# Layer 0's experts in 12 groups instead of 13, the crowded-expert branch in the first group, and the sort in front of the first gather

## Chip, core and metric

The kernel runs on one core of a Trainium2 chip. The metric is device time in microseconds (us) for one execution of the whole program, which computes a two-layer trunk in one launch. Engines are named as in the profile: PE (TensorE matmul), PEld (its weight loads), DVE (VectorE), ACT (ScalarE), POOL (GpSimd) and SP (SyncE, which here issues the DMAs of the weights). A name with a q, as SPq, is the engine's instruction sequencer.

## What is computed

The trunk has two layers. Each layer has a mixer (layer 0: convolution beside differential attention; layer 1: gated linear attention) and then a hierarchical mixture of experts. Layer 0 treats 512 tokens (256 latent, 256 context), layer 1 only the 256 latent ones. The change lies in the mixture of layer 0. Cut to what matters, the reference is

```python
lg = xt @ rg_w + rg_b                       # 4 expert groups
gi = top1(lg); pg = softmax(lg)[gi]
le = (xt @ re_w + re_b)[:, gi, :]           # 8 experts in the chosen group
top_v, top_i = top_k(le, 2)
gate = pg * softmax(top_v)
expert = 8 * gi + top_i                     # two of 32 experts for each token
for e in range(32):                         # rows of e: the tokens routed to it
    h = silu(x_e @ w1[e]) * (x_e @ w3[e])   # w1, w3: 1024 x 512
    y_e = h @ w2[e]                         # w2: 512 x 1024
y[token] += gate * y_e
```

So layer 0 has 1,024 rows to distribute over 32 experts, and every expert's three matrices of 2 MB each (float32) must be read once, whatever number of rows it has.

## The kernel before

**Groups.** The experts of layer 0 are worked off in groups that fill 128 rows. `GROUPS[0]` lists the widths: `PAIR` is two experts of 64 rows, `MIX` is 64, 32 and 32, `QUAD` is four of 32, and one group is (96, 32). There are 13 groups: PAIR, PAIR, (96, 32), MIX, PAIR, MIX, PAIR, MIX, PAIR, MIX, PAIR, MIX, MIX. The first four experts (`E0 = 4`) keep their own numbers, so that their weights can be loaded before the routing is known. The other 28 are sorted by their number of rows, and the widest places go to the fullest experts. Layer 1 has eight groups, all QUAD. A group's width is split into parts (in `parts`): 64 columns in a PAIR, 32 in all others. A matmul of a part uses only the columns of the PE array that belong to it, and parts can run side by side.

**Crowded experts.** An expert with more rows than its place has is finished in a loop, 32 rows in a pass: `rest()` reads the number of passes (`nri`) on every engine, and branches over the loop if it is zero. `crowded()` computes `nri`; in layer 0 it calls `sort()`, which ranks the experts and reorders the table `tab` (slot numbers, gates, counts, expert numbers) with PE transposes and matmuls. `rest()` runs in group `REST[0] = 3`, counted from 0, after that group's down product, whose result is scattered first. Group 0 needs nothing of the sort: its positions `pos0` come from the routing.

**One group.** For group j the program says: `up` (lines 1520 to 1528: x times w1 and w3, 16 steps over k, each with one matmul per part), then the rest of the group's loads, then `act_h` (silu, gate at line 1440, product, four PE transposes), then `prep` of group j + 1 (`group_hot`, `gather`, `gates`: a 0/1 matrix times the tokens, transposed), then `scatter` of group j - 1 (line 1463 on PE, lines 1467 and 1468 on DVE and POOL), then `slots_T` of j + 1, then `down` (lines 1530 to 1537: h times w2), then the first loads of group j + 1, then `split_y`.

**Ring.** A tile of weights is 128 x 2048 float32, 1 MB; an expert has six. `wtile()` hands out places of a ring: four base tiles of the pool `ring` (named wt in the profile), nine that `open_ring` adds and one that `more_ring` adds (wx), 14 in layer 0. The pool has one tag `wt` with four buffers. From the 120th tile on, the index is shifted by one place (`TURN`). The loop body's six loads take six places too, whether it runs or not. `load_group` is a generator: it issues the w1 and w3 loads of a group at its first two steps (four per expert), and the two w2 loads per expert when the caller runs it to its end, after `up`. For sorted experts it first reads the expert's number from `numi` into an SP register (line 1494); lines 1481 and 1483 issue the load for a fixed and for a sorted expert.

**Order.** `TileContext(nc, schedule_with_timeline_sim=True)` lets a planner order the instructions of each engine: by program order as priority, but by its own estimate of when each instruction's inputs are there. So it may put a later group's gather between the matmuls of an up product, or take the parts of a step apart. Nothing is moved over a branch: what the program says before `rest()` stands before it on every engine. Each engine's instructions run in the order in which they were put. `later()` lowers the priority of what stands in it.

**Ahead of the groups.** The last blocks of tokens are modulated by `modulate(b, True)` for b = 2 and 3: ACT, POOL, ACT, and then the low half XL of the split (line 1230), for b = 2 on POOL and for b = 3 on DVE. The routing's DVE chain (lines 1279 to 1338) runs at the same time.

Of the kernel before, what the change touches and what calls it, by code (L numbers as in the profile page):

```python
# [9 lines left out]
FT = mybir.dt.float32  # L10
# [8 lines left out]

D = 1024  # L20
RING = 4
TURN = (120, 1)
LATE = (9, 11)
MORE = (1, 2)

# [1 line left out]

E0 = 4
PAIR, MIX, QUAD = (64, 64), (64, 32, 32), (32,) * 4
GROUPS = ((PAIR, PAIR, (96, 32), MIX, PAIR, MIX, PAIR, MIX, PAIR, MIX, PAIR, MIX, MIX), (QUAD,) * 8)  # L30
REST = (3, 1)
EPS = 1e-6
NE = 32
LAMBDA_INIT = 0.8 - 0.6 * math.exp(0.0)
# [47 lines left out]
def trunk_kernel(ctx: ExitStack, tc: tile.TileContext, A: dict, out: bass.AP):  # L82
    nc = tc.nc
    const = ctx.enter_context(tc.tile_pool(name="const", bufs=1))
    ring = ctx.enter_context(tc.tile_pool(name="ring", bufs=RING))
    psum = ctx.enter_context(tc.tile_pool(name="psum", bufs=1, space=PSUM))
    dram = ctx.enter_context(tc.tile_pool(name="dram", bufs=1, space=bass.MemoryType.DRAM))
    late, ring_at, ring_of = [], [0], []

    def pool(es, name, side):  # L90
        return es.enter_context(tc.tile_pool(name=name, bufs=1, side=side, reuse_waits="tile"))
# [19 lines left out]
    def wtile():  # L111

        if not late:
            return ring.tile([128, 2048], FT, name="wt", tag="wt")
        f = late[(ring_at[0] + TURN[1] * (ring_of[1] == "ring0" and ring_at[0] >= TURN[0])) % len(late)]
        ring_at[0] += 1
        return f()

    def open_ring(es, name, side, n, more=(), order=None):

        f = [lambda: ring.tile([128, 2048], FT, name="wt", tag="wt")] * RING
        for i in range(n):
            p = pool(es, f"{name}{i}", side)
            f.append(lambda p=p: p.tile([128, 2048], FT, name="wx"))
        f += [lambda m=m: m for m in more]
        ring_of[:] = es, name, side
        late[:] = [f[i] for i in order] if order else f
        ring_at[0] = 0
        es.callback(late.clear)
# [1000 lines left out]
    def moe_open(l, nb, side, X):  # L1130
# [88 lines left out]
        def modulate(b, last=False):  # L1219

            x = xs[b]
            if last:
                nc.scalar.activation(x, x, AF.Copy, scale=rs[:, b:b + 1])
                nc.gpsimd.tensor_add(x, x, B2[:, b // 2])
            else:
                nc.vector.scalar_tensor_tensor(x, x, rs[:, b:b + 1], B2[:, b // 2], op0=OP.mult, op1=OP.add)
            t = slice(b * 128, (b + 1) * 128)
            xv = x.rearrange("p (i k) -> p k i", k=8)
            nc.scalar.activation(X[0][:, :, t], xv, AF.Copy)
            (nc.gpsimd if last and b % 2 == 0 else nc.vector).tensor_sub(X[1][:, :, t], xv, X[0][:, :, t].bitcast(FT))  # L1230

        return dict(l=l, nb=nb, ns=ns, es=es, es1=es1, mp=mp, rp=rp, side=side, tab=tab, sub16=sub16, lg=lg, route=route, route_end=route_end, modulate=modulate, X=X, more=[], rs=rs, B2T=B2T if l else None)

    def moe(M):
# [15 lines left out]
        with es:  # L1250
# [93 lines left out]
            with es2:  # L1344
# [141 lines left out]
                def load_group(g):  # L1486

                    W = {}
                    es_ = []
                    p0, m, _ = g  # L1490
                    for x in range(m):
                        e = p0 + x
                        if l == 0 and e >= E0:
                            e = nc.values_load(numi[0:1, e:e + 1], engines=SPE, min_val=0, max_val=NE - 1)
                        es_.append(load_expert(W, e, x))
                    for i, _ in enumerate(zip(*es_)):
                        if i in (0, 4):
                            yield W
                    for i in es_:
                        next(i, None)  # L1500
                    yield W
# [13 lines left out]
                def prep(g, P):  # L1515
                    xgT = ep.tile([128, 8, 128], FT, name="xgT", tag="xgT", bufs=1)
                    gather(P, xgT)
                    return xgT, P, gates(P, g)
# [25 lines left out]
                def sort():  # L1544

                    key, kp, mine = sm[:, 0], sm2[:, 0:1], sm2[:, 1:2]
                    nc.vector.tensor_scalar(num, rev32, -1.0, float(NE), op0=OP.mult, op1=OP.add)

                    nc.vector.scalar_tensor_tensor(key, cnt, 32.0, rev32, op0=OP.mult, op1=OP.add)
                    nc.vector.tensor_scalar(key[:, 0:E0], rev32[:, 0:E0], 1e5, None, op0=OP.add)  # L1550
                    t = sm[:, 1]
                    nc.vector.tensor_mul(t, key, sel4)
                    nc.vector.reduce_sum(kp, t, axis=AX.X)
                    nc.vector.tensor_scalar(t, key, kp, None, op0=OP.is_gt)
                    nc.vector.reduce_sum(mine, t, axis=AX.X)

                    nc.vector.tensor_scalar(mine, mine, 1.0, None, op0=OP.add)
                    nc.vector.tensor_scalar(t, cst[:, C_RK:C_RK + NE], mine, None, op0=OP.is_equal)
                    row = sm2[:, 2:6]
                    nc.vector.reduce_sum(row, ident.rearrange("p (r e) -> p r e", e=NE), axis=AX.X)  # L1560
                    M = ep.tile([128, 512], FT, name="pm", tag="s", bufs=1)[:, 0:128].rearrange("p (r e) -> p r e", r=4)
                    nc.vector.tensor_tensor(M, t[:, None, :].to_broadcast([128, 4, NE]), row[:, :, None].to_broadcast([128, 4, NE]), op=OP.mult)
                    rows_ = 2 * nb + 2
                    tT = ep.tile([128, 512], FT, name="tT", tag="xg", bufs=1)
                    tp = trps()
                    for i in range(0, rows_, 4):
                        n = min(4, rows_ - i) * NE
                        nc.tensor.transpose(tp[0:n, i * 32:i * 32 + 128], tab[:, i:min(i + 4, rows_)].rearrange("p r e -> p (r e)"), ident)
                        nc.vector.tensor_copy(tT[0:n, i * 32:i * 32 + 128], tp[0:n, i * 32:i * 32 + 128])
                    tp = trps()  # L1570
                    for i in range(0, rows_, 4):
                        n = min(4, rows_ - i) * NE
                        nc.tensor.matmul(tp[:, i * 32:i * 32 + n], tT[0:n, i * 32:i * 32 + 128], M.rearrange("p r e -> p (r e)")[0:n, 0:n],
                                         start=True, stop=True)
                    nc.vector.tensor_copy(tab, tp[:, 0:rows_ * NE].rearrange("p (r e) -> p r e", e=NE))
                    nc.vector.tensor_copy(numi, num)
# [101 lines left out]
                def rest():  # L1678

                    n = nc.values_load(nri[0:1, 0:1], min_val=0, max_val=64)  # L1680
                    with tc.If(n > 0):
                        n2 = nc.values_load(nri[0:1, 0:1], min_val=0, max_val=64)
                        with tc.For_i(0, n2):
                            ei, pg = ov_pick()
                            e = nc.values_load(ei[0:1, 0:1], engines=SPE, min_val=0, max_val=NE - 1)
                            W = {}
                            for _ in load_expert(W, e, 1):
                                pass
                            pre = ov_gather(pg)
                            hT2 = ov_up(W, pre)  # L1690
                            scatter(pre[1], split_y(ov_down(W, hT2)))

                NG = len(groups)
                pr = prep(groups[0], group_hot(groups[0], pos0))
                nG = slots_T(pr[1])
                crowded()
                prev = None
                ld = load_group(groups[0])
                for _ in range(2):
# [1 line left out]
                for j, g in enumerate(groups):  # L1701
                    xgT, P, gc = pr
                    G = nG
                    hs = up(W, xgT, g)
                    for _ in ld:
                        pass
                    hT = act_h(hs[0], hs[1], gc)
                    if j + 1 < NG:
                        pr = prep(groups[j + 1], group_hot(groups[j + 1]))
                    if prev is not None:  # L1710
                        scatter(*prev)
                    if j + 1 < NG:
                        nG = slots_T(pr[1])
                    if j == REST[l] and l:
                        rest()
                    ys = down(W, hT, g)
                    if j + 1 < NG:
                        ld = load_group(groups[j + 1])
                        for _ in range(2):
                            W = next(ld)  # L1720
                    prev = (G, split_y(ys))
                    if j == REST[l] and l == 0:
                        scatter(*prev)
                        prev = None
                        rest()
                scatter(*prev)

    moe(mixer0())
# [26 lines left out]
```

## Time and profile before

| | us |
|---|---|
| median of three runs | 1575.86 (1575.17 to 1578.94) |
| the profiled execution | 1574.82 |
| its span | 1573.1 |
| mixer 0 and routing, about | 0 to 347 |
| groups of layer 0 and their scatter, about | 347 to 876 |
| mixer 1, about | 876 to 1140 |
| groups of layer 1, about | 1140 to 1573 |

The page gives the busy time of PE as 1331.3 us (85% of the span), of DVE as 674.0, of ACT as 369.0 and of POOL as 338.7. It moved 498.11 MB, a mean of 317 GB/s. Its second part cuts the span into 40 equal slices of 39.3 us; in the row of GB/s, layer 0's experts are the slices around 295, 400, 376, 213, 324 and then 420 to 424, and layer 1's are the last eleven, at 426 to 427. A busy PE is not PE at its peak.

### The profile page before, as it was taken

The page shows a single profiled execution, that of the slowest core. Times are in us where ns is not written, and L with a number is a line of the kernel's source. Part 1 is how long each engine was busy: PE and PEld are TensorE (multiplying, and loading weights), DVE is VectorE, ACT ScalarE, POOL GpSimd, SP SyncE. Part 2 cuts the span into 40 slices and gives each one's busy share as a digit, 9 for nine tenths or more (in the row PEclk, how much of TensorE's full clock was granted, in tenths as well). Part 3 has the DMA queues.
Part 4 walks back from the last instruction along what each step waited for, and adds up shares of the span by engine and source line. Part 5 has one row for each costly group of instructions (what it writes and reads, how often), then busy time and mean ns, then how long its engine had stood idle before and what let it go on. Part 6 is the DMA issues. An engine that isn't in the chain of part 4 may idle for free. (4 is left out here: it accounts for less than half of the span.)

```text
span 1573.1 us, 19365 instructions
## 1 busy us (share of the span) xinstructions
PE 1331.3 (85%) x7541; PEld 671.3 (43%) x7541; DVE 674.0 (43%) x1301; ACT 369.0 (23%) x706; POOL 338.7 (22%) x234
## 2 busy tenths in 40 slices
PE   5998989859997999999998799988776678778776
PEld 4765647643443434343332487776322122212211
DVE  4589885762245133334334838676202012102121
ACT  3255554531010100001001366444100000000000
POOL 1477402430012011111012545462000000000000
PEclk9999978889997999999999799999798899999998
DMA  9867162377995799999998824468599999999995
GB/s 315 297 222 256 53 215 58 102 299 295 400 376 213 324 422 423 422 423 422 422 404 293 319 88 161 164 216 321 236 426 426 427 427 427 427 427 426 427 427 240
DMA packets 100829, 498.11 MB, mean 317 GB/s; under 512 B 17605, under 2 KB 30248, under 8 KB 45948
## 3 DMA queue, kind: packets, MB, share of 16 engines
q1 hardware_dynamic: 96780, 490.37, 77.9%
q0 software_dynamic: 1680, 6.16, 1.2%
q8 instruction: 61, 1.00, 0.2%
q10 hardware_dynamic: 2272, 0.28, 0.1%
q14 instruction: 36, 0.29, 0.1%
HBM read 495.68 MB, written 1.10 MB: 316 GB/s over the span
## 5 line engine op out<-in xcount | busy, mean ns | idle before, releaser
L1526 PE MATMUL pj<-wx,xgT 128*32 128x512 f32 (+1 forms) x1616 | 330.9, 639 | 59.7 <-DMA wx<-in_moe_w_dram 56.7
L1468 POOL TENSOR_TENSOR H<-H,sc 128x512 f32<-128x512 f32 x68 | 86.7, 1275 | 899.1 <-DVE sc L1467 899.1
L1535 PE MATMUL pj<-wx,hT 128*32 128x512 f32 (+1 forms) x824 | 184.7, 608 | 5.0 <-ACT hT L1445 2.8
L1440 DVE SCALAR_TENSOR_TENSOR s<-s,gc,pj 128x512 f32<-128x512 f32 x21 | 15.7, 747 | 399.6 <-PE pj L1526 328.4
L1526 PEld LDWEIGHTS pj<-wx,xgT 128*32 128x32 f32 (+1 forms) x1616 | 79.8, 120 | 249.0 <-issue 137.8
L1526 PE MATMUL pj<-wt,xgT 128*32 128x512 f32 (+1 forms) x648 | 151.5, 603 | 18.4 <-DMA wt<-in_moe_w_dram 17.7
L370 POOL TENSOR_TENSOR wl<-wt,wh 128x1024 fp32r<-128x1024 f32 x50 | 126.8, 2543 | 144.0 <-ACT wh L369 135.4
L289 PE MATMUL pj<-wh,XH 128*128 128x512 f32 x304 | 123.7, 418 | 15.2 <-ACT p L621 6.8
L290 PE MATMUL pj<-wl,XH 128*128 128x512 f32 x304 | 124.2, 409 | 1.6 <-POOL wl L370 1.6
L1467 DVE TENSOR_TENSOR sc<-wk,g 128x512 f32<-128x512 f32 x136 | 87.6, 686 | 85.5 <-PE wk L1463 83.7
L291 PE MATMUL pj<-wh,XL 128*128 128x512 f32 x304 | 123.6, 408 | 0.2
L1535 PEld LDWEIGHTS pj<-wx,hT 128*32 128x32 f32 (+1 forms) x824 | 44.1, 115 | 94.1 <-issue 81.6
L369 ACT ACTIVATE wh<-wt 128x1024 fp32r<-128x1024 f32 x66 | 69.3, 1056 | 54.4 <-PE pj L291 35.4
L1468 DVE TENSOR_TENSOR H<-H,sc 128x512 f32<-128x512 f32 x68 | 79.6, 1171 | 2.0
L289 PEld LDWEIGHTS pj<-wh,XH 128*128 128x128 f32 x304 | 59.0, 195 | 44.1 <-issue 10.1
L1526 PEld LDWEIGHTS pj<-wt,xgT 128*32 128x32 f32 (+1 forms) x648 | 38.6, 117 | 90.4 <-issue 56.9
L1439 ACT ACTIVATE s<-pj 128x512 f32<-128x512 f32 x21 | 12.5, 597 | 252.4 <-PE pj L1526 245.2
L543 DVE SCALAR_TENSOR_TENSOR wk<-hp,vt,wk 128x512 f32<-128x512 f32 x90 | 67.6, 751 | 1.7
L290 PEld LDWEIGHTS pj<-wl,XH 128*128 128x128 f32 x304 | 59.4, 195 | 16.4 <-POOL wl L370 2.7
L291 PEld LDWEIGHTS pj<-wh,XL 128*128 128x128 f32 x304 | 59.3, 195 | 15.4 <-DVE XL L1094 1.2
L1535 PE MATMUL pj<-wt,hT 128*32 128x512 f32 (+1 forms) x280 | 62.0, 599 | 2.4 <-ACT hT L1445 2.4
L1445 ACT ACTIVATE hT<-trps 128x512 f32<-128x512 f32 x21 | 12.5, 597 | 215.2 <-PE trps L1443 215.2
(461 smaller groups left out, 1982.0 us busy)
## 6 DMA issues: line engine op xcount, KB each, us to landing
wx<-in_moe_w_dram SPq DMA_DIRECT2D x271, 1024.0 KB, 18.6
wt<-in_moe_w_dram SPq DMA_DIRECT2D x102, 1024.0 KB, 19.4
wa<-in_ada_w_dram SPq DMA_DIRECT2D x16, 1024.0 KB, 5.7
wt<-in_gla_w_in_dram SPq DMA_DIRECT2D x12, 1024.0 KB, 6.9
H<-in_moe_w_dram SPq DMA_DIRECT2D x11, 1024.0 KB, 19.6
S<-in_ada_w_dram SPq DMA_DIRECT2D x10, 1024.0 KB, 5.2
wt<-in_ada_w_dram SPq DMA_DIRECT2D x8, 1024.0 KB, 5.3
wt<-in_ab_w_in_dram SPq DMA_DIRECT2D x6, 1024.0 KB, 10.7
```

The costliest lines, as they stand in the source:

```text
L289: nc.tensor.matmul(ps, sh, mh, start=k0, stop=False)
L290: nc.tensor.matmul(ps, sh, ml, start=False, stop=False)
L291: nc.tensor.matmul(ps, sl, mh, start=False, stop=k1)
L369: nc.scalar.activation(wh, w, AF.Copy)
L370: (nc.vector if dve or alt and q % 2 else nc.gpsimd).tensor_sub(wl, w, wh.bitcast(FT))
L543: e.scalar_tensor_tensor(av, hp[:, cb, :, t:t + 256], cw[:, t, cb:cb + 1], av, op0=OP.mult, op1=OP.add)
L1439: nc.scalar.activation(s, h1, AF.Silu)
L1440: nc.vector.scalar_tensor_tensor(s, s, gc, h3, op0=OP.mult, op1=OP.mult)
L1467: nc.vector.tensor_mul(t, ps[:, c], g2[:, b // 2, c])
L1468: (nc.vector if hf else nc.gpsimd).tensor_add(H[:, b, c], H[:, b, c], t)
L1526: nc.tensor.matmul(ps[o:o + w], xgT[:, k, o:o + w], W[nm, x, k // 4][:, k % 4], start=k == 0, stop=k == 7)
L1535: nc.tensor.matmul(ys[hf][o:o + w], hT[:, k, o:o + w], W["2", x, k // 2][:, k % 2, hf * 512:(hf + 1) * 512], start=k == 0, stop=k == 3)
```

## The change

Layer 0 has 12 groups. The two first PAIRs become one QUAD, so the first four fixed experts have places of 32 rows. `REST[0]` becomes 0. In the program, `crowded()` (with the sort) stands behind `group_hot` of group 0 and ahead of its `prep`. `rest()` of layer 0 stands in group 0 behind `act_h` and ahead of group 1's `prep`, with nothing to scatter before it, and the ring's index is set back afterwards to where it stood. The generator of the next group's loads is created earlier, behind `act_h`; its first step is taken where it was, behind `down`. The base tiles of the ring have four tags with one buffer each, handed out in turn, and `TURN` is gone. `load_group` stops after two and four loads per expert instead of none and four. The sort's two scratch tiles are taken from the tag `sc`. The XL half of the last modulated blocks is computed on POOL for both.

```diff
-TURN = (120, 1)
...
-GROUPS = ((PAIR, PAIR, (96, 32), MIX, PAIR, MIX, PAIR, MIX, PAIR, MIX, PAIR, MIX, MIX), (QUAD,) * 8)
-REST = (3, 1)
+GROUPS = ((QUAD, (96, 32), MIX, PAIR, MIX, PAIR, MIX, PAIR, MIX, PAIR, MIX, MIX), (QUAD,) * 8)
+REST = (0, 1)
...
-    ring = ctx.enter_context(tc.tile_pool(name="ring", bufs=RING))
+    ring = ctx.enter_context(tc.tile_pool(name="ring", bufs=1))
...
         if not late:
-            return ring.tile([128, 2048], FT, name="wt", tag="wt")
-        f = late[(ring_at[0] + TURN[1] * (ring_of[1] == "ring0" and ring_at[0] >= TURN[0])) % len(late)]
+            base_at[0] += 1
+            return base(base_at[0] - 1)
         ring_at[0] += 1
-        return f()
+        return late[(ring_at[0] - 1) % len(late)]()
+
+    def base(i):
+        return ring.tile([128, 2048], FT, name="wt", tag=f"wt{i % RING}")
...
-        f = [lambda: ring.tile([128, 2048], FT, name="wt", tag="wt")] * RING
+        f = [lambda i=i: base(i) for i in range(base_at[0], base_at[0] + RING)]
...
-            (nc.gpsimd if last and b % 2 == 0 else nc.vector).tensor_sub(X[1][:, :, t], xv, X[0][:, :, t].bitcast(FT))
+            (nc.gpsimd if last else nc.vector).tensor_sub(X[1][:, :, t], xv, X[0][:, :, t].bitcast(FT))
...
-                        if i in (0, 4):
+                        if i in (2, 4):
                             yield W
...
-                    M = ep.tile([128, 512], FT, name="pm", tag="s", bufs=1)[:, 0:128].rearrange("p (r e) -> p r e", r=4)
+                    M = ep.tile([128, 512], FT, name="pm", tag="sc", bufs=2)[:, 0:128].rearrange("p (r e) -> p r e", r=4)
...
-                    tT = ep.tile([128, 512], FT, name="tT", tag="xg", bufs=1)
+                    tT = ep.tile([128, 512], FT, name="tT", tag="sc", bufs=2)
...
                     n = nc.values_load(nri[0:1, 0:1], min_val=0, max_val=64)
+                    at = ring_at[0]
                     with tc.If(n > 0):
...
+                    if l == 0:
+
+                        ring_at[0] = at
...
-                pr = prep(groups[0], group_hot(groups[0], pos0))
+                P0 = group_hot(groups[0], pos0)
+                crowded()
+                pr = prep(groups[0], P0)
                 nG = slots_T(pr[1])
-                crowded()
...
                     hT = act_h(hs[0], hs[1], gc)
+                    W2 = W
+                    if j + 1 < NG:
+                        ld = load_group(groups[j + 1])
+                    if l == 0 and j == REST[l]:
+                        rest()
                     if j + 1 < NG:
                         pr = prep(groups[j + 1], group_hot(groups[j + 1]))
...
-                    ys = down(W, hT, g)
+                    ys = down(W2, hT, g)
                     if j + 1 < NG:
-                        ld = load_group(groups[j + 1])
                         for _ in range(2):
                             W = next(ld)
                     prev = (G, split_y(ys))
-                    if j == REST[l] and l == 0:
-                        scatter(*prev)
-                        prev = None
-                        rest()
```

More of the change, by code (lines that the diff above doesn't have):

```diff
@@ L84, in trunk_kernel @@
     const = ctx.enter_context(tc.tile_pool(name="const", bufs=1))
-    ring = ctx.enter_context(tc.tile_pool(name="ring", bufs=RING))
+    ring = ctx.enter_context(tc.tile_pool(name="ring", bufs=1))
     psum = ctx.enter_context(tc.tile_pool(name="psum", bufs=1, space=PSUM))
     dram = ctx.enter_context(tc.tile_pool(name="dram", bufs=1, space=bass.MemoryType.DRAM))
-    late, ring_at, ring_of = [], [0], []
+    late, ring_at, ring_of, base_at = [], [0], [], [0]
     def pool(es, name, side):
@@ L1713, in moe @@
                         nG = slots_T(pr[1])
-                    if j == REST[l] and l:
+                    if l and j == REST[l]:
                         rest()
-                    ys = down(W, hT, g)
+                    ys = down(W2, hT, g)
                     if j + 1 < NG:
-                        ld = load_group(groups[j + 1])
                         for _ in range(2):
```

## The prediction

> **What bounds the kernel now.** I read the slices of the page first: layer 0's experts lie at some 350 to 860 us. The windows by stage split that stretch (columns: window, length, busy of PE, its weight loads, DVE, ACT and POOL, granted clock, DMA share, GB/s).
>
> ```profile
> 355.00:490.00 135.00, 132.18 (x801) 57.24 (x797) 43.01 (x79) 16.15 (x27) 11.55 (x9) 1.00 0.92 369
> 490.00:520.00 30.00, 18.50 (x46) 8.79 (x48) 19.04 (x26) 1.57 (x3) 8.89 (x7) 0.60 0.06 25
> 520.00:835.00 315.00, 298.93 (x1586) 121.78 (x1586) 108.55 (x169) 31.28 (x56) 38.29 (x30) 1.00 1.01 419
> ```
>
> Before 490 PE is full and DMA is not. From 490 to 520 both are nearly empty. From 520 both look full, at 419 GB/s, so 2.50 us for a tile of 1.049 MB. Which one leads? PE's waits from 530 to 840 answer it:
>
> ```profile
> PE pj L1526 <- DMA wx<-in_moe_w_dram: 1.6, 2, 1.4
> ```
>
> PE waited 1.6 us in all for weights, so PE sets the pace and the queue is only kept full by it. One row of line 1440 (the gate, once a group, at the end of its up product) marks each group, in the timeline of DVE:
>
> ```profile
> 374.64 0.74 DVE L1440 SCALAR_TENSOR_TENSOR s<-s,gc,pj 128x512 f32<-128x512 f32 x1
> ...
> 404.71 0.75 DVE L1440 SCALAR_TENSOR_TENSOR s<-s,gc,pj 128x512 f32<-128x512 f32 x1 [6.29 <-issue]
> ...
> 472.42 0.75 DVE L1440 SCALAR_TENSOR_TENSOR s<-s,gc,pj 128x512 f32<-128x512 f32 x1 [0.50 <-PE pj L1526]
> ...
> 529.43 0.75 DVE L1440 SCALAR_TENSOR_TENSOR s<-s,gc,pj 128x512 f32<-128x512 f32 x1 [15.65 <-PE pj L1526]
> ...
> 850.25 0.75 DVE L1440 SCALAR_TENSOR_TENSOR s<-s,gc,pj 128x512 f32<-128x512 f32 x1 [7.91 <-PE pj L1526]
> ```
>
> Groups 0 to 3 lie 30.1 us (first step) to 33.9 us (mean of the next two, 67.71 / 2) apart. The step from group 3 to 4, which holds the branch, takes 57.0 us. The eight steps after it take 320.8 us, 40.1 each. Why are groups dearer behind the branch? The down product (line 1535) in three windows of one group each:
>
> ```profile
> 440.00:473.00 33.00, 8.32 (x64) 1.99 (x64) 1.00 0.92 368
> 567.00:606.00 39.00, 11.08 (x64) 2.59 (x64) 1.00 1.01 423
> 804.00:851.00 47.00, 14.87 (x64) 3.21 (x64) 1.00 0.94 389
> ```
>
> The same 64 matmuls took 8.32 us ahead of the branch and 11.08 to 14.87 us behind it. Parts of 32 columns run side by side, four at a time at best; in the trace of the later groups they come three, two or one at a time, in the order in which a planner that expected to wait for weights put them. So a group's price is its order on PE.
>
> What the branch costs shows in SP's timeline, in SP's waits from 460 to 530 and in PE's first row behind it:
>
> ```profile
> 472.91 47.00 SPq L1483 DMA_DIRECT2D wx<-in_moe_w_dram  x4
> 522.44 4.34 SPq L1483 DMA_DIRECT2D wt<-in_moe_w_dram  x4
> ```
> ```profile
> SPq L1483 <- PE pj L1526: 45.3, 7, 30.3
> ```
> ```profile
> 512.93 1.12 PE L1526 MATMUL pj<-wx,xgT 128*64 128x512 f32 x2 [3.00 <-DVEq L1681]
> ```
>
> SP's next load stood 30.3 us for a PE matmul of group 4: the skipped body had taken six places of the ring, so the next place was one that group 4 still needed. PE meanwhile scattered two groups with nothing beside it, then waited 3.00 us for DVE's join.
>
> **The change part by part.** *Path.* It is the chain of PE groups from the first gate (374.64) to the last (850.25), 475.6 us in 12 steps. After, there are 11.
>
> *Two pairs become one quad.* The four steps from 374.64 to 529.43 (154.8 us) become three: quad to (96,32), (96,32) to MIX, MIX to PAIR; what follows is the same sequence of eight steps. The last two stand behind the branch now, so I price them at 40.1 and not at 33.9. That keeps the later sequence at 320.8 us.
>
> The first step starts from 30.1, which also had no scatter to hide. To it come the quad's down product and a dearer up product. Before has no quad in layer 0; layer 1 has only quads, lines 1526 and 1535 there:
>
> ```profile
> 1211.00:1566.00 355.00, 149.23 (x762) 31.67 (x754) 0.92 0.98 412
> ```
> ```profile
> 1211.00:1566.00 355.00, 80.83 (x384) 18.75 (x384) 0.92 0.98 412
> ```
>
> At 128 and 64 matmuls a group these are 6 groups: 24.9 us up (it holds waits for weights) and 13.5 us down. Bounds for the quad's down: 8.3 us as above, and 27 us if its 64 matmuls came singly (28 of them, four abreast, take 3.23 us in a row quoted below, so a step is some 0.43 us). I take 13.5, from the only quads there are, 5.3 more than the 8.2 us of an early group. For the up product I take 1.5 more than the early 15.3, by the row of the first group behind the branch:
>
> ```profile
> 530.00:567.00 37.00, 17.27 (x128) 4.29 (x128) 1.00 1.01 422
> ```
>
> The branch: 3.0 us at the join, as in the row above. Group 1's gather cannot be slipped between group 0's up matmuls any more, since nothing passes a branch; PE has group 0's down product as cover and I add 2.5 us, between 0 and the 7.5 us from the first gather's start (347.26, below) to the first up matmul:
>
> ```profile
> 354.79 3.65 PE L1526 MATMUL pj<-wt,xgT 128*64 128x512 f32 x16 [0.69 <-ACT xgT L1406]
> ```
>
> Sum: 30.1 + 5.3 + 1.5 + 3.0 + 2.5 = 42.4, bounds 33 and 61. Three steps: 42.4 + 80.2 = 122.6, against 154.8: **32.2 us less**.
>
> *The branch moves to group 0 and gives its ring places back.* SP reaches it with 24 loads issued. At the join SP waits for its loads; then come 28 register reads of expert numbers, which may all stand ahead of group 1's loads:
>
> ```profile
> L1494 SPq TENSOR_LOAD <-numi x28: 262/264/472, 374.7 to 394.7; - x28
> L1494 SPq FUSED_REGOPS  x28: 147/147/181, 375.2 to 395.0; - x28
> ```
>
> At 0.264 + 0.147 us each that is 11.5 us of SP. Weights for group 0's down are on their way by then (10 tiles, 25 us), and PE needs group 1's about 40 us after its start; I cost it at nothing. If that cover fails, the 11.5 us are the most it adds, inside the bound of 61.
>
> *The sort stands ahead of the first gather.* Nine PE instructions and a dozen short DVE ones. The sort's matmuls, the XL that POOL has already and the one that moves to it, a DVE row of the same shape, and the gather's start:
>
> ```profile
> L1573 PE MATMUL trps<-pm,tT x6: 272/275/320, 372.2 to 373.6; 128*128 128x128 f32 x4, 64*128 64x64 f32 x2
> ```
> ```profile
> 338.70 2.85 POOL L1230 TENSOR_TENSOR XL<-x,XH 128x1024 fp32r<-128x1024 f32 x1
> ```
> ```profile
> 340.88 2.44 DVE L1230 TENSOR_TENSOR XL<-x,XH 128x1024 fp32r<-128x1024 f32 x1 [2.02 <-ACT XH L1229]
> ```
> ```profile
> L370 DVE TENSOR_TENSOR wl<-wt,wh 128x1024 fp32r<-128x1024 f32 x1 | 1.2, 1224 | 2.9 <-ACT wh L369 2.9
> ```
> ```profile
> 347.26 0.79 PE L1386 MATMUL wk<-XH,P 128*128 128x512 f32 x1 [7.77 <-DVE P L1512]
> ```
>
> Six matmuls and three transposes are about 2.6 us of PE; they leave their old place, which also lay before the first gate. DVE's chain to the gather (347.26) loses the 2.44 us that the second XL took ahead of it. A late sort could hold PE 5 us more; if the gather overlaps it, the start is 2.5 us earlier. I take 0, bounds -3 and +5. [...]
>
> *Ring tags, the removed turn, the earlier creation of the loads.* The generator issues nothing until its first step, which stays behind the down product, so that is nothing. Four base tiles keep their order; at the end of layer 0 other tiles sit in them. Layer 1's first norm waits for the last scatter, not for a load:
>
> ```profile
> 872.28 1.06 ACT L323 ACTIVATE xn<-H 128x1024 f32<-128x1024 f32 x1 [7.25 <-DVE H L1468]
> ```
>
> I take 0, with -4 and +6 as bounds (an SP load that waits for the last down product, against free slots some 8 us earlier).
>
> *Overflow.* All weight loads are
>
> ```profile
> wx<-in_moe_w_dram SPq DMA_DIRECT2D x271, 1024.0 KB, 18.6
> wt<-in_moe_w_dram SPq DMA_DIRECT2D x102, 1024.0 KB, 19.4
> ...
> H<-in_moe_w_dram SPq DMA_DIRECT2D x11, 1024.0 KB, 19.6
> ```
>
> 384, which is 2 x 32 experts x 6: no body ran. Routing the reference's own inputs gives the first four experts 24, 22, 15 and 17 rows, all within 32, so none runs after.
>
> *Sum.* The profiled execution took 1574.82 us (span 1573.1 and 1.7 around it; the median is 1.0 higher). 1574.8 - 32.2 = 1542.6, **1542**.
>
> **The rivals.** *Weights bound layer 0.* If PE kept four abreast (early 33.9 us a group; 11 steps, 373), DMA would lead. [...] From rows:
>
> ```profile
> 358.46 0.80 SPq L1481 DMA_DIRECT2D wt<-in_moe_w_dram  x2
> ```
> ```profile
> 856.00 3.23 PE L1535 MATMUL pj<-wt,hT 128*32 128x512 f32 x28
> ```
>
> SP issued 14 loads ahead of this one; 178 x 2.50 = 445 us from about 360 end at 805, and four more us of down product give 809, against 859.5 now: 50 us less, **1525**. For it: DMA idles 30 us today. Against it: PE never waits for it behind the branch.
>
> *Slower: PE's order gets narrower.* All groups but one stand behind the branch. Break-even is 475.6 / 11 = 43.2 us a step. With the dearest products seen (17.27 up, 14.87 down) in every group a step is 40.1 + 4.8 = 44.9, and 11 of them take 493.9: 18 us more, **1593**. Against it: most later groups were at 11 us down.
>
> *Given back at the seam.* Gains in layer 0, but layer 1's loads wait for slots that now hold the last weights and the sort holds up the first gather: +6 and +5 by the bounds above, **1553**.
>
> *An expert overflows.* A pass costs six loads (15 us) and gather, products and scatter with nothing beside them (the scatter alone took about 20 us in 490 to 512), some 45 us: **1587**. The counts speak against it.
>
> **How the numbers follow.** Forecast 0.58, weights 0.17, seam 0.13, narrower order 0.09 (0.05 of it slower, 0.04 within 0.3%), overflow 0.03. The likeliest case alone spans 1530 to 1556. The range reaches down to the weights' case and up to the bound of the first step (1542 + 19) and a little over: 1520 to 1564. About 0.3%, 4.7 us, is what a measurement of this kernel tells from no change: faster 0.88, within 0.04, slower 0.08.
>
> **What would show it.** Right: 12 rows of line 1440; no stretch of 20 us with DMA near empty between 360 and 800; a first step near 42 us; SP's wait of 30 us gone; the last gate near 818; DMA below full with PE still full. Wrong: PE waiting for weights (the weights' case); steps over 43 us; a hole in DMA behind the join from the register reads; a first gather later than 352; more than 384 weight loads.

## The result and the profile after

The kernel after takes 1552.30 us (median of 4 runs, 1552.09 to 1552.69), the kernel before beside it 1575.51. The ratio is 0.9848 (95% interval 0.9831 to 0.9865), so 23 us less, where 32 were forecast. The forecast was 1542 with a range of 1520 to 1564. The profiled execution after took 1552.13 us, its span 1550.3. Line numbers of the experts' part are two higher than before (the gate is line 1442, the down product 1537).

The slices of the page (DMA share in tenths, then GB/s), after:

```profile
DMA  9857261187999999999998624468799999999995
GB/s 318 290 204 256 92 218 59 55 311 284 422 423 421 422 422 385 424 399 411 355 392 307 228 96 163 164 205 330 285 427 426 427 426 426 427 427 426 427 427 244
```

The hole of the branch (213 in one slice before) is gone; layer 0 has no slice under 355 between 400 and 800 us. The gates, one row a group, in the timeline of DVE: group 0, 1, 3 and the last one.

```profile
376.75 0.75 DVE L1442 SCALAR_TENSOR_TENSOR s<-s,gc,pj 128x512 f32<-128x512 f32 x1 [11.30 <-PE pj L1528]
419.44 0.75 DVE L1442 SCALAR_TENSOR_TENSOR s<-s,gc,pj 128x512 f32<-128x512 f32 x1 [12.43 <-PE pj L1528]
499.45 0.75 DVE L1442 SCALAR_TENSOR_TENSOR s<-s,gc,pj 128x512 f32<-128x512 f32 x1 [16.60 <-PE pj L1528]
827.14 0.75 DVE L1442 SCALAR_TENSOR_TENSOR s<-s,gc,pj 128x512 f32<-128x512 f32 x1 [7.92 <-PE pj L1528]
```

The first three steps take 122.7 us (499.45 - 376.75) in place of four of 154.8: 32.1 less, where 32.2 were forecast; that they agree to 0.1 is luck, since the same kernel in another profile (e12_after below) saves 29.5. But the first gate is 2.1 us later than before, and the last eight steps take 327.7 us in place of 320.8. Together the last gate comes 23.1 us earlier, and that is the whole gain: from it to the end of the span it is 722.9 us before and 723.2 after.

Where do the two losses come from? First, the down product: its line in one window over the whole of layer 0 (window, length, busy PE, weight loads, clock, DMA share, GB/s), before and after.

```profile
340.00:880.00 540.00, 128.05 (x640) 32.92 (x640) 0.95 0.90 368
```
```profile
340.00:860.00 520.00, 146.75 (x640) 35.35 (x640) 0.96 0.96 390
```

As many matmuls, 640, are busy 18.7 us longer. They are not all the same ones, since the quad's 64 stand in place of those of two pairs. The same line over the last eight steps alone, which hold the same eight groups in both, before and after:

```profile
529.43:850.25 320.82, 88.83 (x384) 22.01 (x384) 1.00 1.00 415
```
```profile
499.45:827.14 327.69, 98.36 (x384) 23.93 (x384) 0.99 0.97 399
```

There it is 9.5 us longer, because fewer matmuls stand side by side (the run e6_down_order tests that). The up products of these steps are 2.3 us shorter (127.44 and 125.09), so the two together make the 6.9. Nor is the loss spread over the eight: the first two steps go from 36.9 and 39.1 to 40.1 and 41.0, the last one from 46.5 to 48.1, and the others stay within 0.4 of what they were. The first two are the ones that stood right behind the branch before. Second, the mixer ahead of layer 0. The two XL rows on POOL begin at 345.00 us, 6.3 later than the one before (338.70):

```profile
345.00 5.67 POOL L1232 TENSOR_TENSOR XL<-x,XH 128x1024 fp32r<-128x1024 f32 x2
...
350.62 0.79 PE L1388 MATMUL wk<-XH,P 128*128 128x512 f32 x1 [3.93 <-DVE P L1514]
```

So the mixer is 6.3 us later. From XL's start to the first gather it is 5.6 us and no longer 8.6, and from there to the first gate 26.1 and no longer 27.4: 6.3 - 2.9 - 1.3 = 2.1, the delay of the first gate.

### The profile page after: what moved, and what is told of

It reads as the page before. It is cut to its first block, busy times and chain, and to the rows that moved or that the text cites. A ratio compares the mean times of both kernels' runs of the same rounds, so it can differ in the third digit from the quotient of the medians.

```text
span 1550.3 us, 19208 instructions
## 1 busy us (share of the span) xinstructions
PE 1312.0 (85%) x7485; PEld 656.1 (42%) x7485; DVE 659.3 (43%) x1283; ACT 366.0 (24%) x699; POOL 336.7 (22%) x231
## 5 line engine op out<-in xcount | busy, mean ns | idle before, releaser
L1528 PE MATMUL pj<-wx,xgT 128*32 128x512 f32 (+1 forms) x1608 | 312.5, 639 | 55.9 <-DMA wx<-in_moe_w_dram 55.9
L1470 POOL TENSOR_TENSOR H<-H,sc 128x512 f32<-128x512 f32 x64 | 81.4, 1273 | 865.8 <-DVE sc L1469 865.8
L1442 DVE SCALAR_TENSOR_TENSOR s<-s,gc,pj 128x512 f32<-128x512 f32 x20 | 14.9, 747 | 435.7 <-PE pj L1528 389.1
L1537 PE MATMUL pj<-wx,hT 128*32 128x512 f32 (+1 forms) x848 | 193.3, 616 | 6.8 <-ACT hT L1447 4.6
L1528 PEld LDWEIGHTS pj<-wx,xgT 128*32 128x32 f32 (+1 forms) x1608 | 76.0, 119 | 243.1 <-issue 135.4
L1469 DVE TENSOR_TENSOR sc<-wk,g 128x512 f32<-128x512 f32 x128 | 82.5, 686 | 68.5 <-PE wk L1465 66.7
L1470 DVE TENSOR_TENSOR H<-H,sc 128x512 f32<-128x512 f32 x64 | 73.2, 1144 | 1.8
L1537 PE MATMUL pj<-wt,hT 128*32 128x512 f32 (+1 forms) x256 | 69.7, 620 | 4.2 <-issue 1.8
L1528 PEld LDWEIGHTS pj<-wt,xgT 128*32 128x32 f32 (+1 forms) x656 | 36.2, 119 | 85.8 <-issue 52.8
```

The source lines that it names most:

```text
L1442: nc.vector.scalar_tensor_tensor(s, s, gc, h3, op0=OP.mult, op1=OP.mult)
L1469: nc.vector.tensor_mul(t, ps[:, c], g2[:, b // 2, c])
L1470: (nc.vector if hf else nc.gpsimd).tensor_add(H[:, b, c], H[:, b, c], t)
L1528: nc.tensor.matmul(ps[o:o + w], xgT[:, k, o:o + w], W[nm, x, k // 4][:, k % 4], start=k == 0, stop=k == 7)
L1537: nc.tensor.matmul(ys[hf][o:o + w], hT[:, k, o:o + w], W["2", x, k // 2][:, k % 2, hf * 512:(hf + 1) * 512], start=k == 0, stop=k == 3)
```

## The experiments

My theory A at this point: the gain is what was forecast (the removed stall and one group less), and two things give part of it back: the four base tags, which change the order of the mixer's loads, and the order of the down products on PE. Each run stood beside the kernel before on the same chip; the last column is the difference to that.

| kernel | edit to the kernel after | us, median (range) | against before |
|---|---|---|---|
| e12_after | none (control) | 1553.45 (1552.26 to 1556.90) | -21.6 |
| e4_pair_pair | 13 groups | 1575.04 (1572.15 to 1579.97) | +0.7 |
| e5_no_branch | no branch in layer 0 | 1550.12 (1543.56 to 1555.32) | -24.2 |
| e8_no_return | ring places kept by the body | 1558.46 (1553.65 to 1560.33) | -16.1 |
| e2_xl_dve | one XL back on DVE | 1554.24 (1551.73 to 1556.75) | -20.3 |
| e3_sort_behind | sort behind the first gather | 1554.48 (1552.78 to 1555.21) | -20.1 |
| e1_one_tag | one ring tag | 1544.47 (1543.63 to 1545.91) | -29.9 |
| e6_down_order | down product in written order | 1531.88 (1529.43 to 1535.17) | -42.5 |
| e7_down_tag | e6 and e1 | 1521.78 (1520.33 to 1525.39) | -52.8 |
| e9_both_tag | e7, up product too | 1525.41 (1522.50 to 1530.53) | -49.7 |
| e10_13_down_tag | e7 with 13 groups | 1550.21 (1549.62 to 1551.62) | -24.9 |
| e11_before_down | kernel before, down in written order | 1563.48 (1561.82 to 1566.78) | -11.6 |

**The control.**

> The kernel after, unchanged, to stand beside the others on the same chip. Both theories: 1550 to 1555, the first gate of layer 0 at 376 to 382.

Both hold: 1553.45, first gate at 378.77. The same kernel on another chip is 1 us off, so differences of 2 us between kernels on different chips say nothing.

**The number of groups.**

```diff
-GROUPS = ((QUAD, (96, 32), MIX, ...
+GROUPS = ((PAIR, PAIR, (96, 32), MIX, ...
```

> The kernel after, with two groups of two experts in place of the first group of four, so 13 groups again; the branch still stands in the first one and gives its ring places back. The weights are the same 384 loads. Theory A (a group costs its PE time): one step of 37 to 42 us more and a first group dearer by less, the last gate 27 to 38 us later than 827.1, time 1580 to 1588. Rival (the weights set the pace, and the number of groups does not matter; the gain came from the removed stall alone): the last gate within 10 us of 827.1, time 1550 to 1562.

The first and the last gate of this kernel:

```profile
376.88 0.75 DVE L1442 SCALAR_TENSOR_TENSOR s<-s,gc,pj 128x512 f32<-128x512 f32 x1 [9.11 <-PE pj L1528]
854.38 0.75 DVE L1442 SCALAR_TENSOR_TENSOR s<-s,gc,pj 128x512 f32<-128x512 f32 x1 [7.92 <-PE pj L1528]
```

The last gate is 27.2 us later, at the low edge of theory A and far from the rival's 10. The time, 1575.04, is not 1580, since the stretch behind the last gate is 716.6 us here (span 1571.0) and not 723; why that stretch is shorter is not shown. The weights are the same, so a group costs PE time. And this kernel is no faster than before (+0.7): its first four steps take 151.7 us where they took 154.8, and its last eight 325.8 where they took 320.8. So the wait of 30 us is gone, but the groups around it became dearer by nearly as much, and the gain of the whole change is here that of the group less. (The tags, below, give back some more; what they cost with 13 groups was not run.) The last eight steps are as dear as with 12 groups, so their order does not come from the number of groups.

**The branch, left out.**

```diff
-                    if l == 0 and j == REST[l]:
-                        rest()
```

> The kernel after without the branch of layer 0: the rows that an expert has beyond its places are not computed (with these inputs there are none). Theory A (the narrow order comes from the planner's guess at the weights, not from the branch; the branch costs the join and what cannot be slipped past it): the first step falls from 42.7 to 33 to 38 us, the later ones stay at 39 to 41, time 1543 to 1549. Rival (the branch is what makes the order behind it narrow): the later down products fall to about 8.3 us, steps to 34 to 37, time 1505 to 1530. Second rival (weights pace the layer): the first step falls, the later ones give it back, time 1550 to 1552.

The first step is 37.9 us (gates at 379.05 and 416.94), inside A's 33 to 38. The later steps are 39.9 to 41.1 us, one 36.8 and the last 46.5, much as in the kernel after (39.0 to 41.0, one 36.7, the last 48.1), and the down products are busy 140.62 us in all. So the first rival falls: the order is nearly as narrow without any branch. The second falls too: the last eight steps take 326.4 us against 326.2 in the control, so they do not give back what the first step gains. The times spread over 12 us in four runs and do not settle what the branch costs; the steps say 5 us (37.9 against 42.7), 7 against the control's 45.3.

**The ring places, not given back.**

```diff
-                    if l == 0:
-                        ring_at[0] = at
```

> The kernel after, but the skipped body of the branch keeps the six ring places that it drew, as it did before the change; the branch stays in the first group. Theory A (the stall of before came from these places, wherever the branch stands): the load that follows the branch waits 10 to 25 us for a matmul of the first or second group, the queue shows a hole of 10 us or more behind the join, the later order on PE is as in the kernel after, and the time is 1555 to 1572. Rival (the place of the branch is what mattered, since at the first group the ring has slack): no hole beyond 5 us and the time is 1552 within 3.

One window behind the join, the kernel after and this one (last: DMA share, GB/s):

```profile
360.00:400.00 40.00, 35.66 (x225) 14.81 (x218) 7.29 (x21) 4.87 (x7) 0.00 (x0) 0.96 0.89 365
```
```profile
360.00:400.00 40.00, 33.56 (x211) 14.86 (x211) 8.63 (x26) 5.46 (x8) 0.00 (x0) 0.91 0.65 264
```

The queue stands still for a further quarter of these 40 us, and the first step is 50.4 us in place of 42.7 (control: 45.3). SP's first load behind the branch starts at 402.02 us, against 389.78 in the control. Its longest single wait for a down matmul is 8.9 us, a little under theory A's 10 to 25. The time is 5 us above the control. So the cause is as theory A had it, at or under its low end: the six places cost some 5 us at this place of the branch.

**XL and the sort.**

```diff
-            (nc.gpsimd if last else nc.vector).tensor_sub(X[1]...
+            (nc.gpsimd if last and b % 2 == 0 else nc.vector).tensor_sub(X[1]...
```

> The kernel after, with the second of the two late subtractions (XL, line 1232) back on VectorE. Theory A (the loss ahead of layer 0 is that of the tags alone): the mixer's times stay as in the kernel after, VectorE's chain to the first gather gets its 2.4 us back, the first gate falls at 376 to 380 against 376.75, and the time is 1551 to 1556. Rival (GpSimd's second subtraction costs the mixer its time, or holds VectorE's sort up): the first gate falls 3 us or more earlier and the time is 1546 to 1549.

```profile
346.40 2.86 POOL L1232 TENSOR_TENSOR XL<-x,XH 128x1024 fp32r<-128x1024 f32 x1
348.59 2.45 DVE L1232 TENSOR_TENSOR XL<-x,XH 128x1024 fp32r<-128x1024 f32 x1 [2.02 <-ACT XH L1231]
355.11 0.80 PE L1388 MATMUL wk<-XH,P 128*128 128x512 f32 x1 [3.35 <-DVE P L1514]
```

The mixer is as late as after, so XL did not delay it. From POOL's XL to the first gather it is 8.7 us with one XL on DVE, and 5.6 with both on POOL. So the XL that moved to POOL is a gain of 3 us at that place (the control has 5.6 as well, 346.46 to 352.07); undone, it puts the first gate to 381.72, past A's 380, and the rival, which had it earlier, falls. In the time 1 us is left of it, too little to tell.

```diff
...
-                crowded()
                 pr = prep(groups[0], P0)
                 nG = slots_T(pr[1])
+                crowded()
```

> The kernel after, with the counting and the sort back behind the first gather, and their scratch tiles in their old tags; the branch stays in the first group. Theory A (the sort ahead of the gather costs no more than a few us, since its short instructions lie beside the load of the first weights): the first gather starts 0 to 4 us earlier, the first gate falls at 373 to 378 against 376.75, and the time is 1549 to 1554. Rival (behind the gather the numbers and the count come late, and the branch waits for them): the first step is 46 us or more in place of 42.7 and the time is 1554 to 1562.

XL to first gather is 5.60 us (343.18 to 348.78), as with the sort ahead, so the sort in front costs the gather nothing. With the sort behind it the first step is 47.4 us, inside the rival's range, but only 2 us above the control's 45.3. Part of that is PE's clock, which was at half for 13.7 us there and for 10.2 us in the control (last section). The time is at the border of the two ranges, 1 us above the control, so this run does not decide between them.

**The ring tags.**

```diff
-    ring = ...tile_pool(name="ring", bufs=1)
+    ring = ...tile_pool(name="ring", bufs=RING)
...
-        return ring.tile([128, 2048], FT, name="wt", tag=f"wt{i % RING}")
+        return ring.tile([128, 2048], FT, name="wt", tag="wt")
```

> The kernel after, but all base tiles of the ring drawn from one tag of four rotating buffers, as before. Theory A (the four fixed tags change the order in which the planner issues the mixer's loads, and cost mixer 0 some 6 us): the loads between 30 and 65 us come as before, the mixer's PE rows stand where they stood before (the x loads of the experts at 310.9 and not 317.2), the first gate of layer 0 falls 2 to 6 us earlier than 376.8, and the time is 1546 to 1550 against 1552.3. Rival (the mixer is later because of the subtraction that went to GpSimd or of the sort): the mixer stays 3 to 6 us late and the time is 1552 within 1. In both, the eight last steps of layer 0 stay near 327 us.

SP's timeline of loads early in the mixer, first with one tag, then the kernel after:

```profile
29.46 8.62 SPq L229 DMA_DIRECT2D wt<-in_ada_w_dram  x4
38.18 7.39 SPq L359 DMA_DIRECT2D wt<-in_ab_w_in_dram  x4
```
```profile
29.35 3.00 SPq L229 DMA_DIRECT2D wt<-in_ada_w_dram  x2
32.45 3.20 SPq L359 DMA_DIRECT2D wt<-in_ab_w_in_dram  x1
35.74 5.66 SPq L229 DMA_DIRECT2D wt<-in_ada_w_dram  x2
41.49 2.09 SPq L359 DMA_DIRECT2D wt<-in_ab_w_in_dram  x1
```

With four tags the planner puts one of the `ab_w_in` tiles in between those of `ada_w`, and the next one stands at 41.49 and no longer right behind 38.18. PE's rows are equal in both kernels up to 45 us; from 60 on those of the kernel after are 3.1 us later. At 290 to 300 a second loss comes, in a wait of PE for ACT in the attention (one tag, then after):

```profile
292.23 0.79 PE L291 MATMUL pj<-wh,XH 128*128 128x512 f32 x1 [6.57 <-ACT p L623]
```
```profile
300.79 0.79 PE L291 MATMUL pj<-wh,XH 128*128 128x512 f32 x1 [10.07 <-ACT p L623]
```

PE is 7.5 us late by 310; how the tags lead to this second loss is not shown. With one tag the first gate is at 369.81, the time 1544.47: 8 us less, more than A's range. The rival falls. The last eight steps are 326.5 us.

**The order of the down product.** Each matmul of a down product of layer 0 is put behind the one that the program writes before it; this orders the issue and adds no wait for completion.

```diff
+                def chain(prev, ins):
+                    if l == 0 and prev is not None:
+                        tc.add_manual_dep(ins.ins, prev.ins.name, ...NoSync...)
+                    return ins
...
-                                nc.tensor.matmul(ys[hf][o:o + w], ...
+                                q = chain(q, nc.tensor.matmul(ys[hf][o:o + w], ...
```

> The kernel after, with the matmuls of each down product of layer 0 tied to the order in which the program writes them, so that the parts of a step stand side by side. Nothing else is changed. Theory A (the order of the down product on PE sets the pace in layer 0, weights stand ready): the down products take 7 to 8.5 us a group in place of 10 to 15, the eight last steps take 295 to 312 us in place of 327.7, and the time is 1532 to 1540. Rival (the weights set the pace as much as PE: the queue ran at 421 GB/s from 420 to 580): the down products get shorter just so, but PE waits for weights in their place, the eight steps stay within 320 to 328 and the time is 1547 to 1552.

The down product's line over layer 0, and the last gate:

```profile
340.00:860.00 520.00, 119.03 (x640) 27.33 (x640) 0.95 0.97 399
```
```profile
804.15 0.75 DVE L1442 SCALAR_TENSOR_TENSOR s<-s,gc,pj 128x512 f32<-128x512 f32 x1 [7.86 <-PE pj L1533]
```

119.0 us in place of 146.75 (9.9 a group, not quite the 7 to 8.5 that I had expected), the last eight steps 308.1, the time 20 to 21 us less. Theory A holds and the rival falls. Who leads shows in SP's waits from 400 to 800 (total, times, longest), the kernel after and this one:

```profile
SPq L1485 <- PE pj L1528: 127.1, 46, 8.4
SPq L1485 <- PE pj L1537: 122.9, 32, 10.3
SPq L1485 <- DMA wx<-in_moe_w_dram: 45.2, 25, 2.1
SPq L1485 <- DMA wt<-in_moe_w_dram: 14.3, 9, 2.2
```
```profile
SPq L1485 <- DMA wx<-in_moe_w_dram: 191.5, 101, 2.6
SPq L1485 <- DMA wt<-in_moe_w_dram: 79.8, 44, 2.5
SPq L1485 <- PE pj L1533: 34.8, 24, 4.5
SPq L1485 <- PE pj L1543: 9.4, 10, 4.7
```

After, SP stood 250 us for ring places that PE still used, and 60 for transfers. With the down product mended it is 44 and 271: the queue is now full, and the loads wait mainly for it. That it alone sets the pace is not shown: PE still shows next to no wait for weights (1.7 us from 380 to 830), and a group more costs its PE time here too (e10_13_down_tag).

**Both together, and the up product.**

> The kernel after with the down product of layer 0 in its written order and the base tiles in one rotating tag, the two edits that each made it faster by themselves (20 us and 8 us). With the first of them alone the queue ran at 421 to 424 GB/s from 400 to 800, so the weights lead there. Theory A (in the weights' hold of layer 0 an earlier start of the loads is still worth its whole time): 1523 to 1527. Rival (the two gains are the same slack): 1530 to 1533.

1521.78 us, a ratio of 0.9667 (0.9653 to 0.9680) to before: the fastest kernel of this study, 31 us below the kernel after. It lies 1 us under theory A's range and far from the rival's. The two gains add up (20 and 8; 10 of the tags on top of the first).

> As e7_down_tag, with the up product of layer 0 held to its written order too. Theory A (with the down product mended the queue is full from 400 to 800 and the weights lead): the same as e7_down_tag within 3 us, 1519 to 1525. Rival (PE still leads): the two dozen narrow steps of the up products vanish and the time falls to 1508 to 1516.

1525.41, on another chip. The steps from gate to gate are those of e7_down_tag within 0.1 us, and the up products are busy as long (183.15 and 183.17 us), so the edit did not change the order of the up products: a repeat, and no test of the rival.

**A group where the queue is full.**

> As e7_down_tag, but with 13 groups as in e4_pair_pair. With the old order a group more cost 23 us. In e7_down_tag PE has some 23 us of idle time between 400 and 800 (377.34 busy) and the queue none. Theory A (a group more costs only where PE leads; here it takes its 33 us out of that slack): 1524 to 1536, so 2 to 14 us more than e7_down_tag. Rival (a group more costs its PE time whatever leads): 1541 to 1548.

1550.21, 28 us above e7_down_tag: in neither range, but beyond the rival's and far from theory A's. I had read PE's idle time in e7_down_tag as slack. The window and PE's waits there, 400 to 800:

```profile
400.00:800.00 400.00, 377.34 (x2226) 152.81 (x2222) 155.25 (x234) 40.42 (x72) 57.11 (x45) 1.00 1.01 422
```
```profile
PE trps L1445 <- DVE s L1442: 10.5, 11, 1.0
PE wk L1465 <- DVE sc L1469: 7.5, 16, 0.5
PE pj L1543 <- ACT hT L1447: 3.8, 11, 0.7
PE wk L1388 <- DVE sc L1469: 0.9, 2, 0.5
```

10.5 + 7.5 + 3.8 + 0.9 = 22.7 us is all of its idle time: short waits for DVE and ACT in the chain of each group, which the group more did not fill. PE and the queue are both at their ends there. With 13 groups SP's loads wait for PE alone again (2.2 us of other waits, on PE too, stand below these):

```profile
SPq L1485 <- PE pj L1533: 162.3, 55, 8.4
SPq L1485 <- PE pj L1543: 152.0, 38, 11.9
```

**The kernel before, with the order mended.**

> The kernel before, with the down product of layer 0 in its written order and nothing else changed; the branch stands behind the fourth group and keeps its ring places. Theory A (with the order mended the weights lead, and the hole of some 30 us in the queue at the branch is then lost for good): 1545 to 1556, and 24 to 34 us more than e7_down_tag, which has the same tags, so the whole change without the tags would be worth more there than the 23 us that it gave. Rival (the order was all that made before slow, and the hole is made up behind the branch): 1526 to 1540.

1563.48, 12 us less than before, and in neither range. The last eight steps take 306.2 us in place of 320.8, the four ahead 154.7 as before. The hole at the branch is still there and is not made up; what A's range missed fits the 13th group, which costs its chain on PE here too (28 us between e10 and e7).

```profile
480.00:520.00 40.00, 28.20 (x110) 13.43 (x112) 22.81 (x32) 1.57 (x3) 10.19 (x8) 0.70 0.29 117
```

From this kernel to e7_down_tag, which have the same tags and the same rule for the down product, it is 41 us (differences to before): 13 for the rest of the change, that is the branch with its places, the sort, XL, the turn and the order of the loads (e11 to e10, one chip), and 28 for the group.

## Why the prediction came out as it did

- **PE sets the pace, and a group is worth its PE time**: right. A group more costs 22 us with the old order (e4 against the control) and 28 with the mended one (e10 against e7).
- **First step 42.4**: 42.7 in the profile of the result, but 45.3 in the control's. Inside the bounds; the agreement to 0.3 us is luck, and so is that of its terms. The quad's down product was priced at 13.5 us and took 13.64. But the up product of this step was priced at 16.8 and took 13.92, so the rest of what was added, the join and the gather by its terms, came to 8.4 and not 5.5. **Next two steps 40.1 each**: 39.0 and 41.0. Sum of the three -32.2: measured -32.1, in the control -29.5.
- **"That keeps the later sequence at 320.8"**: this term was mis-sized, 327.7 (326.2 in the control, where the last step does not have the clock at half). The eight groups behind are the same, but the planner put their down products narrower still: 98.4 us in place of 88.8. The rival of a narrower order came true to that extent. Its counter, that most later groups stood at 11 us of down product, was misread: of the eight, two stood at 7.3, three at 11.1, two at 13.0 and one at 14.9. e6 shows that the order costs this time: with it tied down the same steps take 308.1.
- **Ring tags at nothing, since "four base tiles keep their order"**: this step failed. The tiles keep their order, the planner does not: it issues the loads of the mixer otherwise, and PE is 6 us later at layer 0 than before (7.5 later than with one tag). e1 shows 8 us in the time. The bounds of -4 and +6 stood at the seam behind layer 0, and the loss came ahead of it.
- **Sort and XL at nothing, -3 to +5**: XL brought 3 us (e2), and the sort in front cost the gather nothing (e3). DVE's XL took 2.05 and 2.15 us before (at 296.42 and 299.00, with no work on POOL) and 2.44 us at 340.88, begun 0.67 us ahead of the end of POOL's XL: 0.3 to 0.4 us more.
- **Register reads hidden, no hole behind the join**: right; from 384 to 400 us the queue ran at 419 and 420 GB/s in the rows below.
- **Seam 0**: right, 722.9 against 723.2 us behind the last gate. The rival that gave the gain back there was right in its sum, 1553, and wrong in its place.
- **Overflow**: none; 384 loads:

```profile
wx<-in_moe_w_dram SPq DMA_DIRECT2D x274, 1024.0 KB, 19.5
wt<-in_moe_w_dram SPq DMA_DIRECT2D x99, 1024.0 KB, 12.1
...
H<-in_moe_w_dram SPq DMA_DIRECT2D x11, 1024.0 KB
```

- **Weights lead, 1525**: not in the kernel after. With the down product held in order and one tag the queue is full and the time, 1521.78, is near the rival's; but PE is full there as well (e10), so it is not shown that the weights lead.

In sum: -32.1 (three steps) + 6.9 (order of the last eight) + 2.1 (first gate: mixer +6.3, XL -2.9, the way to the gate -1.3) = -23.1. In the control's profile it is -29.5 + 5.4 + 4.1 = -20.0. Left open: why the planner writes the down products narrower. It is not that a branch stands in the layer (e5), nor the number of groups (e4) or the tags (e1: 326.5). The branch no longer stands right ahead of these eight groups, which fits the two steps that became longer; no run tests that, nor the turn and the order of the loads. Open is also what shortens the end in e4_pair_pair.

## What to carry to other kernels

Where a planner orders an engine by its own estimate, an edit of tiles or tags anywhere can reorder a stage far away: compare the order of every stage and not only of the edited one, and where an order is known to be good, tie it down (20 us here). To see whether a queue is full, read whom the loads wait for, not whether the engine waits: PE showed next to no wait for weights both when the loads stood 250 us for it and when they stood 271 us for transfers. A full queue does not show that the engine beside it has time to spare: a group more still cost 28 us. Idle time that is all made of short waits in each group's chain is part of the group's price, not slack.

## What the hardware showed beside that

The first step of one and the same kernel was 42.7 us in one profile and 45.3 in another. The window from 384 to 392 us, right behind the join (busy PE is the third column, the granted clock the third from the end), in the profile of the result and in the control's:

```profile
384.00:392.00 8.00, 6.86 (x25) 3.84 (x26) 0.69 (x1) 1.19 (x2) 0.00 (x0) 1.00 1.02 419
392.00:400.00 8.00, 8.00 (x47) 4.27 (x46) 1.99 (x7) 0.60 (x1) 0.00 (x0) 1.00 1.01 420
```
```profile
384.00:392.00 8.00, 5.78 (x11) 3.32 (x12) 0.00 (x0) 0.00 (x0) 0.00 (x0) 0.50 1.01 414
```

In the control PE worked at half its clock there. In the profile of the result it did so as well, but earlier and for a shorter time. The 3.4 us ahead of the drop, and the drop, in the profile of the result and in the control's:

```profile
375.98:379.39 3.41, 1.65 (x8) 0.70 (x8) 1.48 (x4) 0.60 (x1) 0.00 (x0) 1.00 1.00 418
379.39:382.80 3.41, 3.18 (x6) 0.35 (x2) 0.10 (x1) 0.00 (x0) 0.00 (x0) 0.50 1.01 416
```
```profile
378.66:382.07 3.41, 1.65 (x10) 0.83 (x10) 1.58 (x4) 0.60 (x1) 0.00 (x0) 1.00 1.01 425
382.07:392.31 10.24, 7.96 (x16) 3.69 (x14) 0.00 (x0) 0.00 (x0) 0.00 (x0) 0.50 1.01 415
```

So half clock lasted 3.4 us in one execution and 10.2 us, three times as long, in the other. The first step is 2.6 us longer there, and 6.8 us more at half clock can account for up to 3.4, by an estimate (6.8 x 0.50). Without the branch (e5_no_branch) PE had full clock:

```profile
384.00:392.00 8.00, 8.00 (x46) 4.96 (x42) 2.30 (x8) 0.79 (x2) 0.00 (x0) 1.00 1.01 421
```

With the branch in the first group half clock lasted 3.4 us around the join (kernel after), 6.8 (e6_down_order), 10.2 (the control) or 13.7 (e3_sort_behind). Each of these lengths is near a whole multiple of 3.4 us. In the 3.4 us ahead of either drop above PE was busy for 1.65. What brings the clock down, and for how long, no run here shows.
